# A hybrid SSD and attention encoder layer on one core: token statistics, V, dt and K at the start of the kernel

## The chip, the cores and the metric

The kernel runs on one core of one Trainium2 chip. Five engines work side by side and are tied together by semaphores: TensorE (PE in the profile, its weight loads PEld), VectorE (DVE), ScalarE (ACT), GpSimd (POOL) and SyncE (SP), which here only issues DMAs. The metric is the time of one execution on the device, in microseconds (us); lower is better. The time of a kernel is the median over its runs.

## The reference

One layer over 512 tokens of width 1024, in float32. Only its beginning matters here:

```python
h = rmsnorm(x, pre_mix_norm[l])          # x * rsqrt(mean(x*x) + EPS) * g
proj = h @ w_in[l]
z, xbc, dt_raw, q, k, v, gates = split_cols(proj, IN_SPLITS)
...
dt = jax.nn.softplus(dt_raw + dt_bias)   # 512 tokens x 64 (2 directions x 32 heads)
...
mixed = (g_ssd * y_ssd + g_attn * y_attn) @ w_o[l]
x = x + rmsnorm(mixed, post_mix_norm[l])
f = jnp.square(jax.nn.relu(rmsnorm(x, pre_mlp_norm[l]) @ w_mlp_in[l])) @ w_mlp_out[l]
x = x + rmsnorm(f, post_mlp_norm[l])
```

`rmsnorm` multiplies a token by one number of its own, r = rsqrt(mean(x*x) + EPS), and a channel by its gain g. Since r belongs to the token, (x * g * r) @ w equals ((x * g) @ w) * r: the factor can be put on before the product or after it. V has 256 columns, dt 64, K 256, Q 1024. The state-space scan and the windowed attention, two projections, a merge, an output projection and the MLP follow; they are most of the work, and nothing in them is changed.

## The kernel before

Every large product is one of float32 matrices in three passes: an operand is split into a high part `hi` (rounded to the format that TensorE multiplies in one pass, fp32r in the profile) and a low part `lo = x - hi`, and the helper `mm3` issues hi·hi, hi·lo and lo·hi into one PSUM bank. A plain float32 product (`mm` on unsplit operands) is also possible; TensorE makes it in several passes and it leaves two records in the trace for one instruction. Weights come by DMA into three buffers `wr` of 128x1024, ScalarE rounds them into `wh`, and GpSimd (for the first weights, DVE and GpSimd) subtracts to give `wl`; `wh` and `wl` have three buffers each too. Token tiles are 128x512, channels on the partitions: `h` holds, for each of the eight blocks k of 128 channels, the high and the low part of the normalised tokens. PSUM has eight banks, three with the tag `pp` and five with the tag `ps`.

The program is a list of quanta, each a product with the weight chunks it needs, and `at` hangs other work on a place in that list. When all is recorded, `Planner` sets the order of every engine's instructions: it simulates the program with a cost for each kind of instruction, takes TensorE's work in the order of the quanta (except that it may pick another ready product), and the others' by their due times; `chain` then ties the instructions of each engine together in that order. The order does not change at run time. SP may have eight DMAs under way; a further one waits for the landing of the one eight places earlier.

The start, around which the change lies:

- Eight products of ones keep TensorE busy while the first loads arrive.
- Tokens 0 to 255 come transposed from the host (`in_xt`, channels first, in five loads), and are multiplied by the gains into `xg` (L697 on ScalarE, L699 on DVE). The first quantum (`plain`) multiplies them, unsplit, with the raw V and dt weights `wr`: 16 plain float32 products of 320 columns, eight for each block of 128 tokens. Their result is multiplied by r at its eviction (L629, L630).
- All 512 tokens come once more as rows (`in_x`, eight loads of 128x512), because r needs the sum over a token's row: ScalarE and DVE sum the squares (L723, L724), GpSimd takes the power (L726, L727). Tokens 256 to 511 are scaled as rows and transposed on TensorE (16 products, L454) in `start_tokens`, then split with the gain into `h` (L475, L476). Their V and dt come from `rest`: 48 split products of 320 columns.
- Tokens 0 to 255 get their r in `scale_tokens`: GpSimd writes a diagonal matrix `dg` of r (L737), TensorE multiplies ones with it so that r stands in every partition of a bank (`rb`), DVE multiplies (L743), ScalarE rounds (L745) and GpSimd subtracts (L746) into `h`.
- Two K products follow (24 split products of 512 columns each, from `h`), then Q products of the same size, then the scores of the first head, which need K (`KH`, `KL`) and Q. K is split from its bank by `k_done`: L886 and L888 on ScalarE, L887 on DVE.
- `dt_math` makes the softplus of dt as |v|, exp, a reciprocal (L826), a product with it (L827) and a polynomial (L831 to L834), all in SBUF tiles of 128x256 called `dtw`.

Of the kernel before, what the change touches and what calls it, by code (L numbers as in the profile page):

```python
# [49 lines left out]
X_CHUNKS = ((0, 1), (1, 3), (3, 5), (5, 7), (7, 8))  # L50
COLD = 7000.0
RATE, EARLY, LAND = 260, 350, 2500
# [26 lines left out]
def packed(given):  # L79

    rows = lambda n: given[n].reshape(-1, 128)
    xt, wv = given["x"][0, :256].T.reshape(8, 128, 256), np.concatenate(
        [given["w_in"][0][:, c:c + n].reshape(8, 128, n) for c, n in ((C_V, 256), (C_DT, 64))], axis=2)
    pieces = lambda a, cuts: np.concatenate([a[k0:k1].transpose(1, 0, 2).reshape(-1) for k0, k1 in cuts])
# [9 lines left out]
    first = np.concatenate([rows("pre_mix_norm").T, xt[0]], axis=1)  # L94
    return {**{n + "_b": blocks(a) for n, a in mats.items()}, "cv": np.ascontiguousarray(cv), "row": row, "bias": bias,
            "xt": np.concatenate([first.reshape(-1), pieces(xt, X_CHUNKS[1:])]), "wv": pieces(wv, V_CHUNKS)}
# [21 lines left out]
class Planner:  # L118
# [191 lines left out]
    def plan(self, wait=0.3):  # L310
# [13 lines left out]
        for _ in self.ins:  # L324
# [22 lines left out]
            if e == "SP" or "DMA" in type(self.ins[n]).__name__:  # L347
                aps = self.operands(self.ins[n].outs)
                size = 4 * math.prod(d[1] for d in aps[0].ap)
                queue = max(queue, t + 900) + size / (EARLY if t < 12000 else RATE)  # L350
# [38 lines left out]
class Trunk:  # L389
# [206 lines left out]
    def v_quanta(self):  # L596
# [5 lines left out]
        self.dtv = get("dtw", (128, 4, 64))  # L602

        def chunk(k0, k1):
            kk = k1 - k0
            raw = []

            def loads():
                r = self.wp.tile([128, 1024], F32, tag="wr", name=self.name("wr"), bufs=RAW)
                self.tags[r.tensor.name] = "wr", RAW  # L610
                raw.append(r[:, :kk * 320].rearrange("p (k n) -> p k n", k=kk))
                (nc.sync if k0 else nc.scalar).dma_start(
                    r[:, :kk * 320], self.d_wv[k0 * 320 * 128:k1 * 320 * 128].rearrange("(p n) -> p n", p=128))

            def make():
                hi, lo = (t[:, :kk * 320].rearrange("p (k n) -> p k n", k=kk) for t in self.weight_parts())
                nc.scalar.copy(hi, raw[0])
                for k in range(kk):
                    e = nc.vector if k % 2 == 0 else nc.gpsimd
                    e.tensor_tensor(lo[:, k], raw[0][:, k], hi[:, k].bitcast(F32), op=ALU.subtract)  # L620
# [4 lines left out]
        def done(t, ps):  # L625
            bias = self.row[:, :64]
            if t < 2:
                r = self.rst0[:, t:t + 1]
                nc.scalar.activation(self.V[0][:, t], ps[:, :256], AF.Copy, scale=r)  # L629
                nc.vector.scalar_tensor_tensor(self.dtv[:, t], ps[:, 256:320], r, bias, op0=ALU.mult, op1=ALU.add)  # L630
            else:
                nc.scalar.copy(self.V[1][:, t - 2], ps[:, :256])
                nc.vector.tensor_tensor(self.dtv[:, t], ps[:, 256:320], bias, op=ALU.add)

        held, late = [], []

        def plain(parts):
            held.extend(parts)
            ps = [self.bank("ps") for _ in range(2)]
            for (k0, k1), (raw, _, _) in zip(V_CHUNKS, parts):  # L640
                for t in range(2):
                    for k in range(k0, k1):
                        self.mm(ps[t][:, :320], self.xg[k][:, tok(t)], raw[:, k - k0], k == 0, k == 7)
            for t in range(2):
                done(t, ps[t])

        def rest(c):
            def run(_):
                if c == 0:
                    late.extend(self.bank("ps") for _ in range(2))  # L650
                (k0, k1), (_, wh, wl) = V_CHUNKS[c], held[c]
                for t in (2, 3):
                    for k in range(k0, k1):
                        hi, lo = self.h[k]
                        self.mm3(late[t - 2][:, :320], (hi[:, tok(t)], lo[:, tok(t)]), (wh[:, k - k0], wl[:, k - k0]),
                                 k == 0, k == 7)
                if c == 2:
# [8 lines left out]
    def start(self):  # L666
# [21 lines left out]
        for x, (k0, k1) in zip(xt, X_CHUNKS):  # L688
# [3 lines left out]
            if k0 == 0:  # L692
                nc.vector.tensor_copy(self.gT, x[:, :8])
# [1091 lines left out]
```

## Time and profile before

| what | us |
|---|---|
| three runs | 1074.57, 1074.58, 1075.67 |
| median | 1074.58 |
| the profiled execution, whole | 1077.91 |
| its span, from the first to the last instruction of the program | 1076.1 |
| TensorE busy in that span | 1064.1 |

TensorE is busy for 99% of the span, at a granted clock of 0.998 of full speed. Its share of busy time says little of the others: DVE is at 71%, ScalarE at 61%, GpSimd at 74%. The 1.8 us between the span and the whole profiled execution lie around the program. The profiled execution is 3.3 us longer than the median of the runs; a difference worked out in its trace is taken over to the runs as it is.

How to read the rows that follow: a row of the timeline has the start and the duration in us, the engine, the line, the operation, what it writes and reads, the shape, how many instructions are merged in the row, and in brackets the idle time of that engine before it and what ended it. A row of the groups has, behind the bar, the busy time in us and the mean duration of one in ns, and then idle time. A row of the waits of TensorE has who waited for whom, the total in us, how often, and the longest. A row of the windows has the stretch, its length, and for each engine the busy time and the number of instructions.

### The profile page before, as it was taken

The page shows a single profiled execution, that of the slowest core. Times are in us where ns is not written, and L with a number is a line of the kernel's source. Part 1 is how long each engine was busy: PE and PEld are TensorE (multiplying, and loading weights), DVE is VectorE, ACT ScalarE, POOL GpSimd, SP SyncE. Part 2 cuts the span into 40 slices and gives each one's busy share as a digit, 9 for nine tenths or more (in the row PEclk, how much of TensorE's full clock was granted, in tenths as well). Part 3 has the DMA queues.
Part 4 walks back from the last instruction along what each step waited for, and adds up shares of the span by engine and source line. Part 5 has one row for each costly group of instructions (what it writes and reads, how often), then busy time and mean ns, then how long its engine had stood idle before and what let it go on. Part 6 is the DMA issues. An engine that isn't in the chain of part 4 may idle for free.

```text
span 1076.1 us, 16654 instructions
## 1 busy us (share of the span) xinstructions
PE 1064.1 (99%) x5542; PEld 895.0 (83%) x5542; DVE 769.1 (71%) x1363; ACT 657.7 (61%) x1409; POOL 797.6 (74%) x993
## 2 busy tenths in 40 slices
PE   9999999999999999999999999999999999999997
PEld 7788888888888888888888888889888888888885
DVE  5877778797786878788876626698663574574688
ACT  7676786786676767676777524466555444444552
POOL 5755548566677789899979976215587898898995
PEclk9999999999999999999999999999999999999999
DMA  8243324434434425254545544317221431424222
GB/s 290 90 140 92 119 91 116 131 98 110 124 123 122 152 89 186 84 142 143 147 128 153 161 154 155 108 53 271 89 69 60 156 97 61 157 90 151 73 98 78
DMA packets 61509, 133.20 MB, mean 124 GB/s; under 512 B 9064, under 2 KB 18920, under 8 KB 61424
## 3 DMA queue, kind: packets, MB, share of 16 engines
q1 hardware_dynamic: 61136, 131.76, 39.4%
q8 instruction: 43, 0.70, 0.3%
q14 instruction: 42, 0.34, 0.1%
q10 hardware_dynamic: 288, 0.39, 0.1%
HBM read 127.63 MB, written 4.49 MB: 123 GB/s over the span
## 4 chain that ended last, share of the span: by engine, by line
PE 91%; DVE 4%; ACT 2%; issue 1%; DMA 1%; POOL 0%; SPq 0%; DVEq 0%; POOLq 0%; ACTq 0%
PE pp L450 57%; PE ps L450 31%; PE ps L454 3%; DVE dtw L827 1%; DMA wr<-in_wv 1%; DVE u L1015 0%; ACT P L947 0%; DVE P L938 0%; DVE dtw L831 0%; PE pp L454 0%; DVE KL L887 0%; DVE P L953 0%; ACT h L745 0%; DVE x L1417 0%; DVE Q L914 0%
## 5 line engine op out<-in xcount | busy, mean ns | idle before, releaser
L529 POOL TENSOR_TENSOR wl<-wr,wh 128x256 fp32r<-128x256 f32 (+1 forms) x519 | 417.0, 835 | 168.7 <-ACT wh L525 166.0
L450 PE MATMUL pp<-h,wh 128*128 128x512 f32 (+1 forms) x1728 | 524.7, 385 | 1.2 <-ACT KH L888 1.2
L450 PEld LDWEIGHTS pp<-h,wh 128*128 128x128 f32 x1728 | 318.5, 188 | 63.2 <-ACT KH L888 1.6
L450 PE MATMUL pp<-h,wl 128*128 128x512 f32 (+1 forms) x864 | 333.9, 386 | 0.0
L525 ACT CAST wh<-wr 128x1024 fp32r<-128x1024 f32 (+1 forms) x130 | 135.4, 1041 | 126.5 <-PE pp L450 98.1
L450 PEld LDWEIGHTS pp<-h,wl 128*128 128x128 f32 x864 | 162.4, 188 | 31.9 <-issue 0.3
L1622 POOL TENSOR_TENSOR wl<-wd,wh 128x256 fp32r<-128x256 f32 x158 | 131.6, 870 | 11.9 <-ACT wh L1619 11.8
L1619 ACT CAST wh<-wd 128x512 fp32r<-128x512 f32 x92 | 53.2, 618 | 38.3 <-PE ps L450 22.1
L450 PE MATMUL ps<-wl,fh 128*128 128x512 f32 x184 | 71.7, 390 | 0.0
L450 PE MATMUL ps<-wh,fl 128*128 128x512 f32 x184 | 71.6, 389 | 0.0
L450 PE MATMUL ps<-wh,fh 128*128 128x512 f32 x184 | 71.6, 389 | 0.0
L1457 DVE SCALAR_TENSOR_TENSOR pp<-pp,r 128x256 f32<-128x256 f32 (+1 forms) x31 | 17.3, 559 | 65.5 <-ACT r L1454 65.4
L1181 ACT ACTIVATE n<-cb,tables 128x128 f32<-128x128 f32 x128 | 47.6, 391 | 16.4 <-DVE cb L1172 12.6
L1015 DVE SCALAR_TENSOR_TENSOR u<-pp,cv,u 128x510 f32<-128x510 f32 (+1 forms) x64 | 47.8, 746 | 9.7 <-ACT u L1011 8.4
L1220 POOL TENSOR_TENSOR w<-w,E 128x256 f32<-128x256 f32 x48 | 40.5, 859 | 16.3 <-DVE w L1216 15.3
L1182 ACT ACTIVATE m<-cb,tables 128x128 f32<-128x128 f32 x128 | 47.5, 389 | 7.2 <-DVE cb L1172 6.4
L1113 POOL TENSOR_TENSOR xd<-x,tables 128x256 f32<-128x256 f32 x48 | 32.5, 696 | 17.0 <-ACT x L1038 15.4
L1177 ACT ACTIVATE rf<-rf,tables 128x128 f32<-128x128 f32 x128 | 42.3, 392 | 3.3 <-DMA rf<-csT 3.2
L1175 POOL TENSOR_TENSOR rb<-rb,tables 128x512 f32<-128x512 f32 x32 | 36.5, 1142 | 10.0 <-DVE al L468 5.9
L947 ACT ACTIVATE P<-P,mx 128x384 f32<-128x384 f32 (+1 forms) x64 | 35.2, 552 | 14.0 <-DVE mx L944 14.0
L1674 DVE TENSOR_TENSOR acc<-acc,ps 128x512 f32<-128x512 f32 x46 | 31.3, 681 | 15.7 <-PE ps L450 15.5
L1183 DVE TENSOR_TENSOR m<-m,n 128x512 f32<-128x512 f32 x32 | 29.6, 925 | 16.0 <-ACT m L1182 15.5
(291 smaller groups left out, 2215.0 us busy)
## 6 DMA issues: line engine op xcount, KB each, us to landing
wr<-in_w_in_b SPq DMA_DIRECT2D x74, 512.0 KB, 3.9
wr<-in_w_mlp_in_b SPq DMA_DIRECT2D x32, 512.0 KB, 3.4
wd<-in_w_mlp_out SPq DMA_DIRECT2D x64, 256.0 KB, 4.5
rb<-csT SPq DMA_DIRECT2D x32, 256.0 KB, 3.8
rf<-csT SPq DMA_DIRECT2D x32, 256.0 KB, 3.8
wr<-in_w_ssd_out_b SPq DMA_DIRECT2D x13, 512.0 KB, 3.6
x<-in_x SPq DMA_DIRECT2D x16, 256.0 KB, 5.2
E<-csE SPq DMA_DIRECT2D x32, 128.0 KB, 4.5
```

Source lines behind the costliest of these rows:

```text
L450: self.nc.tensor.matmul(out, lhsT, rhs, start=start, stop=stop, skip_group_check=more)
L525: self.nc.scalar.copy(hi[:, :m], raw)
L529: engines[e].tensor_tensor(lo[:, c], raw[:, c], hi[:, c].bitcast(F32), op=ALU.subtract)
L947: nc.scalar.activation(p[:, :w], p[:, :w], AF.Exp, bias=mx[:, n:n + 1], accum_out=sm[:, n:n + 1])
L1015: nc.vector.scalar_tensor_tensor(u[:, a:e], ps[:, a + d:e + d], self.wtap(t, b), u[:, a:e], op0=ALU.mult, op1=ALU.add)
L1175: nc.gpsimd.tensor_tensor(v4(rb), v4(rb), cs[:, 1].unsqueeze(2).to_broadcast([128, 4, 128]), op=ALU.subtract)
L1177: nc.scalar.activation(v4(rf)[:, h], v4(rf)[:, h], AF.Identity, bias=ncs[:, 0, h:h + 1])
L1181: nc.scalar.activation(v4(n)[:, h], cb[:, 0], AF.Copy, scale=dt[:, 0, h:h + 1])
L1182: nc.scalar.activation(v4(m)[:, h], cb[:, 1], AF.Copy, scale=dt[:, 1, h:h + 1])
L1220: nc.gpsimd.tensor_tensor(wc, wc, E[:, d], op=ALU.add)
L1619: nc.scalar.copy(hi, src)
L1622: (nc.vector if q == 512 else nc.gpsimd).tensor_tensor(lo[:, c], src[:, c], hi[:, c].bitcast(F32), op=ALU.subtract)
```

## The change

Seven edits, all within the start:

1. All 512 tokens come transposed from the host: eight loads of 128x512 (`xt`), one for each block of 128 channels. The gains travel with the first V and dt weights, which come in four loads instead of three (`W_CHUNKS`).
2. ScalarE and DVE split each transposed block, multiplied by the gain but not by r, into a second set of operands `hr` (hi and lo, all 512 tokens; `raw_tokens`). The transposes on TensorE and `start_tokens` are gone.
3. V and dt of all four token blocks come from `hr`: for the first channel block by four plain products (`PLAIN = 1`), for the other seven by 84 split ones; all four banks are multiplied by r at their eviction. The V weights are rounded block by block.
4. The K products read `hr` too. `k_done` first multiplies the bank by r into a tile `kf` on DVE, and splits K from there.
5. `scale_tokens` now makes `h` for all 512 tokens: four `dg` on DVE instead of two on GpSimd; DVE multiplies each `xt` by its gain and the bank `rb` (128x512), ScalarE rounds, and GpSimd (even k, two halves) or DVE (odd k, whole) subtracts. It is placed after the V products, and `rb` is also copied to SBUF for K.
6. The identity, which `dg` needs, is now issued on SP after the first weights of K instead of on ScalarE at the beginning.
7. In `dt_math` the tiles `e` and `s2` lie in a PSUM bank, and one step writes to another tile than before; the computation is the same.

The planner's numbers for early DMAs change with it (350 to 370 bytes per ns, up to 20 us instead of 12 us).

```diff
-V_CHUNKS = ((0, 2), (2, 5), (5, 8))
-X_CHUNKS = ((0, 1), (1, 3), (3, 5), (5, 7), (7, 8))
+W_CHUNKS = ((0, 1), (1, 2), (2, 5), (5, 8))
+PLAIN, SCALE_AT = 1, 2.5
...
+        def product(k0, k1):
+            def run(parts):
+                if k0 == 0:
+                    banks.extend(self.bank("ps") for _ in range(4))
+                raw, wh, wl = parts[0]
+                for k in range(k0, k1):
+                    for t in range(4):
+                        ps = banks[t][:, :320]
+                        if k < PLAIN:
+                            self.mm(ps, self.xg[k][:, tok(t)], raw[:, k - k0], k == 0, k == 7)
+                        else:
+                            hi, lo = self.hr[k]
+                            self.mm3(ps, (hi[:, tok(t)], lo[:, tok(t)]), (wh[:, k - k0], wl[:, k - k0]), k == 0, k == 7)
+                if k1 == 8:
+                    for t in range(4):
+                        done(t, banks[t])
                     self.dt_math()
...
-        self.at(0, lambda: nc.scalar.dma_start(self.ident, self.d_cst[:, :128]))
+        self.at(0, lambda: nc.sync.dma_start(self.ident, self.d_cst[:, :128]))
...
+    def raw_tokens(self):
+        nc = self.nc
+        for k, x in enumerate(self.xt):
+            g = self.gT[:, k:k + 1]
+            if k < PLAIN:
+                for c in (slice(0, 256), slice(256, 512)):
+                    nc.vector.tensor_scalar(self.xg[k][:, c], x[:, c], self.g0 if k == 0 else g, None, op0=ALU.mult)
+            hi, lo = self.hr[k]
+            self.split_by(hi, lo, x, g)
+        for t in range(4):
+            xt = self.load_tokens(t)
+            self.token_scale(t, xt)
...
-        for t in range(2):
+        for t in range(4):
             dg = get("dg", (128, 128))
-            nc.gpsimd.tensor_scalar(dg, self.ident, self.rst0[:, t:t + 1], None, op0=ALU.mult)
+            nc.vector.tensor_scalar(dg, self.ident, self.rst0[:, t:t + 1], None, op0=ALU.mult)
             self.mm(rb[:, t * 128:(t + 1) * 128], ones, dg, True, True)
...
+        self.rb = get("rb")
+        nc.scalar.copy(self.rb, rb)
         for k in range(8):
...
+            x = self.xt[k]
+            hi, lo = self.h[k]
+            nc.vector.scalar_tensor_tensor(x, x, self.gT[:, k:k + 1], rb, op0=ALU.mult, op1=ALU.mult)
             nc.scalar.copy(hi, x)
...
+            for e, c in ((nc.vector, slice(0, 512)),) if k % 2 else ((nc.gpsimd, slice(0, 256)), (nc.gpsimd, slice(256, 512))):
+                e.tensor_tensor(lo[:, c], x[:, c], hi[:, c].bitcast(F32), op=ALU.subtract)
...
-        w = [self.dtv] + [get("dtw", (128, 4, 64)) for _ in range(5)]
-        v, e, r, s2, p, al = w
+        w = [self.dtv] + [get("dtw", (128, 4, 64)) for _ in range(3)]
+        v, r, p, al = w
+        bank = self.bank("ps")
+        e, s2 = (bank[:, a:a + 256].rearrange("p (c h) -> p c h", c=4) for a in (0, 256))
...
         def k_done(ps):
+            x = get("kf")
+            nc.vector.tensor_tensor(x, ps, self.rb, op=ALU.mult)
             for j in range(2):
...
-                nc.scalar.copy(KH[a], ps[a])
-                nc.vector.tensor_tensor(KL[a], ps[a], KH[a].bitcast(F32), op=ALU.subtract)
+                nc.scalar.copy(KH[a], x[a])
+                nc.vector.tensor_tensor(KL[a], x[a], KH[a].bitcast(F32), op=ALU.subtract)
...
-        hh = lambda: self.h
+        hh = lambda: self.hr
```

Where the order moves. First place, the beginning of the program on TensorE: the products behind the ones, before (`ps` banks of tokens 0 to 127 and 128 to 255, raw weights `wr`):

```order
L450 MATMUL pp_82<-ones_80 128x128 x8
L450 MATMUL ps_177<-wr_153,xg_113 128x320
L450 MATMUL ps_178<-wr_153,xg_113 128x320
L450 MATMUL ps_177<-wr_153,xg_113 128x320
L450 MATMUL ps_178<-wr_153,xg_113 128x320
L450 MATMUL ps_177<-wr_155,xg_114 128x320 x2
```

and after (four banks, one for each 128 tokens; `hr_109` and `hr_110` are the high and low part of the second channel block):

```order
L452 MATMUL pp_82<-ones_80 128x128 x8
L452 MATMUL ps_229<-wr_142,xg_132 128x320
L452 MATMUL ps_230<-wr_142,xg_132 128x320
L452 MATMUL ps_231<-wr_142,xg_132 128x320
L452 MATMUL ps_232<-wr_142,xg_132 128x320
L452 MATMUL ps_229<-wh_150,hr_109 128x320
L452 MATMUL ps_229<-wl_151,hr_109 128x320
L452 MATMUL ps_229<-wh_150,hr_110 128x320
```

Split products now stand where plain ones stood, from the fifth product on, and need ScalarE's and DVE's parts there.

On SP the loads between the tokens' rows and the constants, before (`row` is dt's bias and other small vectors, broadcast; `wr` the weights of K and Q):

```order
L715 DMA x_142<-in_x 128x512
L435 DMA row<-in_row 128x176
L505 DMA wr_199<-in_w_in_b 128x1024
L505 DMA wr_312<-in_w_in_b 128x1024
L921 DMA bt_501<-in_bias 128x384
```

and after:

```order
L709 DMA x_220<-in_x 128x512
L507 DMA wr_249<-in_w_in_b 128x1024
L667 DMA ident<-in_cst 128x128
L507 DMA wr_251<-in_w_in_b 128x1024
L507 DMA wr_299<-in_w_in_b 128x1024
L437 DMA row<-in_row 128x176
```

The identity stands behind the first weights of K, and `row` behind those of K and of the first Q product.

Second place, the softplus and K on DVE. Before (`dtw_376` is e, `dtw_377` the reciprocal, `pp_409` the first K bank, `dtw_71` dt before the softplus):

```order
L743 TENSOR_TENSOR hf_271<-pp_261,xg_116 128x256 x2
L633 TENSOR_TENSOR dtw_71<-ps_299,row 128x64
L826 RECIPROCAL dtw_377<-dtw_377 128x256
L827 TENSOR_TENSOR dtw_376<-dtw_376,dtw_377 128x256
L887 TENSOR_TENSOR KL_435<-pp_409,KH_434 64x512
L887 TENSOR_TENSOR KL_441<-pp_409,KH_440 64x512
L831 SCALAR_TENSOR_TENSOR dtw_379<-dtw_379,dtw_378 128x256 x5
```

After (`ps_358` is the bank of e and s2; `pp_378` the bank `rb`; `h_94`, `h_98`, `h_102`, `h_106` the low parts of odd channel blocks):

```order
L739 SCALAR_TENSOR_TENSOR xt_131<-xt_131,gT,pp_378 128x512
L742 TENSOR_TENSOR h_94<-xt_125,h_93 128x512
L742 TENSOR_TENSOR h_98<-xt_127,h_97 128x512
L742 TENSOR_TENSOR h_102<-xt_129,h_101 128x512
L639 SCALAR_TENSOR_TENSOR dtw_71<-ps_232,rst_79,row 128x64
L742 TENSOR_TENSOR h_106<-xt_131,h_105 128x512
L860 TENSOR_TENSOR kf_458<-pp_433,rb_391 128x512
L803 RECIPROCAL dtw_355<-dtw_355 128x256
L804 TENSOR_TENSOR ps_358<-ps_358,dtw_355 128x256
L866 TENSOR_TENSOR KL_461<-kf_458,KH_460 64x512
L809 SCALAR_TENSOR_TENSOR dtw_356<-dtw_356,ps_358 128x256 x6
```

Four subtractions of 128x512 with both operands in SBUF stand ahead of K and the softplus; the subtraction for `KL` reads SBUF instead of a bank.

On GpSimd at the same place, before:

```order
L737 TENSOR_SCALAR dg_265<-ident,rst_79 128x128
L529 TENSOR_TENSOR wl_315<-wr_199,wh_314 128x256 x4
L746 TENSOR_TENSOR h_92<-hf_268,h_91 128x256
L746 TENSOR_TENSOR h_94<-hf_268,h_93 128x256
L746 TENSOR_TENSOR h_96<-hf_269,h_95 128x256
```

and after (`wl_254` and `wl_302` are K's, `wl_424` and `wl_475` those of the first two Q products):

```order
L531 TENSOR_TENSOR wl_254<-wr_249,wh_253 128x256 x4
L531 TENSOR_TENSOR wl_302<-wr_251,wh_301 128x256 x4
L742 TENSOR_TENSOR h_92<-xt_124,h_91 128x256 x2
L531 TENSOR_TENSOR wl_424<-wr_299,wh_423 128x256
L742 TENSOR_TENSOR h_96<-xt_126,h_95 128x256 x2
L531 TENSOR_TENSOR wl_424<-wr_299,wh_423 128x256
L742 TENSOR_TENSOR h_100<-xt_128,h_99 128x256 x2
L531 TENSOR_TENSOR wl_424<-wr_299,wh_423 128x256
```

K's low parts come first now, and `h` is made between the weights of the first Q product. Behind the scores of the first head, TensorE's products stand in the same order in both programs to the end.

154 lines of the change are left out of this document (51 added, 103 removed).

## The prediction

> **What bounds the kernel now.** I read the page first, then TensorE's waits, then its windows, then the timeline of the first 50 us.
>
> ```profile
> span 1076.1 us, 16654 instructions
> ...
> PE 1064.1 (99%) x5542; PEld 895.0 (83%) x5542; DVE 769.1 (71%) x1363; ACT 657.7 (61%) x1409; POOL 797.6 (74%) x993
> ```
>
> ```profile
> PE pp L450 <- ACT KH L888: 1.2, 1, 1.2
> PE ps L450 <- DVE pT L964: 1.1, 1, 1.1
> ...
> PE ps L450 <- DVE Q L914: 0.3, 1, 0.3
> ```
>
> ```profile
> 4.62:25.27 20.65, 20.08 (x102) 15.79 (x102) 14.18 (x36) 15.41 (x36) 12.22 (x19) 1.00 0.85 313
> 25.27:49.00 23.73, 22.24 (x98) 17.75 (x96) 18.29 (x22) 15.04 (x28) 17.51 (x25) 1.00 0.26 88
> 49.00:1076.10 1027.10, 1018.24 (x5330) 857.84 (x5330) 736.03 (x1302) 625.12 (x1345) 767.68 (x947) 1.00 0.39 121
> ```
>
> Behind each stretch stand its length and TensorE's busy time. TensorE bounds the kernel from 5 us to the end. From the first head's scores (49.00) on its order is the same in both programs, so the change is worth what it moves that moment; the 1027.1 us behind it are taken over unchanged. Two stretches lie ahead: to the first K product (25.27), and two K and two Q products to the scores.
>
> ```profile
> 1.04 3.79 PE L450 MATMUL pp<-ones 128*128 128x128 f32 x16 [1.04 <-DVE two L675]
> 4.62 10.33 PE L450 MATMUL ps<-wr,xg 128*128 128x320 f32 x32
> 15.14 0.44 PE L454 MATMUL pp<-ident,x 128*128 128x128 f32 x2 [0.20 <-ACT x L760]
> ...
> 16.78 0.38 PE L454 MATMUL ps<-ident,x 128*128 128x128 f32 x2
> ...
> 20.28 0.46 PE L450 MATMUL ps<-wh,h 128*128 128x320 f32 x2
> ...
> 22.04 0.46 PE L450 MATMUL ps<-wh,h 128*128 128x320 f32 x2
> ...
> 22.77 0.61 PE L450 MATMUL pp<-dg,ones 128*128 128x128 f32 x4
> ...
> 25.27 0.62 PE L450 MATMUL pp<-h,wh 128*128 128x512 f32 x2
> ...
> 49.00 0.39 PE L450 MATMUL ps<-KH,Q 128*128 128x256 f32 x1 [0.30 <-DVE Q L914]
> ```
>
> ```profile
> 5.15 0.34 PEld L450 LDWEIGHTS ps<-wr,xg 128*128 128x128 f32 x1 [0.20 <-issue]
> 5.68 0.34 PEld L450 LDWEIGHTS ps<-wr,xg 128*128 128x128 f32 x1 [0.20 <-issue]
> ```
>
> A plain product of 320 columns takes 0.53 us (5.15 to 5.68), a split one 0.147 (twelve between 20.28 and 22.04). The first stretch holds 16 x 0.53 = 8.5, the transposes (15.14 to 17.1) 2.0, 48 x 0.147 = 7.1 and two `dg` products, at most 0.6: 18.2 us of work in 20.65; the other 2.4 are waits for loads and for r. In the second stretch 1.5 us are waits (1.2 and 0.3). Their cause:
>
> ```profile
> 29.93 8.42 POOL L529 TENSOR_TENSOR wl<-wr,wh 128x256 fp32r<-128x256 f32 x12
> 30.02 1.75 DVE L826 RECIPROCAL dtw<-dtw 128x256 f32<-128x256 f32 x1 [1.64 <-ACT dtw L825]
> ...
> 31.81 7.17 DVE L827 TENSOR_TENSOR dtw<-dtw,dtw 128x256 f32<-128x256 f32 x1
> ...
> 38.90 0.67 DVE L887 TENSOR_TENSOR KL<-pp,KH 64x512 fp32r<-64x512 f32 x1
> 39.61 0.58 ACT L888 CAST KH<-pp 64x512 fp32r<-64x512 f32 x1 [7.14 <-DVE KL L887]
> ```
>
> L827 takes 7.17 us and ends when GpSimd's unbroken run of twelve subtractions (0.70 each) is over. K's low part stands behind it on DVE, ScalarE behind that, and TensorE lacks the next rounded weights.
>
> **The change: TensorE's own work.** Twelve plain products go (6.4 us), 36 split ones come (5.3); the transposes go (2.0), two `dg` products come (at most 0.6). 15.7 against 18.2: 2.5 us less, certain as far as TensorE stays the bound.
>
> **Loads.** The rows of the windows give what the DMAs moved.
>
> ```profile
> 0.00:5.00 5.00, 3.96 (x17) 3.92 (x18) 0.87 (x6) 2.20 (x3) 0.41 (x5) 1.00 0.64 197
> 5.00:10.00 5.00, 4.86 (x15) 2.97 (x14) 3.13 (x6) 2.46 (x5) 2.12 (x2) 1.00 1.01 373
> 10.00:15.00 5.00, 4.94 (x19) 3.17 (x17) 3.51 (x9) 3.95 (x9) 2.82 (x5) 1.00 1.05 386
> 15.00:20.00 5.00, 4.62 (x32) 4.04 (x33) 4.31 (x14) 4.70 (x14) 3.33 (x7) 1.00 1.03 397
> ```
>
> ```profile
> 13.58 0.63 ACT L723 ACTIVATE junk<-x 128x512 f32<-128x512 f32 x1 [0.63 <-DMA x<-in_x]
> 14.12 0.18 ACT L723 ACTIVATION_READ_ACCUMULATOR junk<-x 128x1 f32 x1
> 14.36 0.72 ACT L760 ACTIVATE x<-x,rst 128x512 f32<-128x512 f32 x1
> ```
>
> 0.98 MB are moved by 5 us, 2.85 by 10, 4.78 by 15, 6.77 by 20. ScalarE waits until 13.57 for the fifth load of rows; by the queue's order 3.74 MB stand up to its end, but 4.23 had been moved, so a load lands when 0.49 MB more than its place in the queue have gone. After: the transposed tokens are 2.10 MB, the V weights 1.31, the rows 2.10, K's first weights 0.52, the identity 0.07. SP's limit of eight holds each load until the one eight places ahead has landed, which keeps some 2 MB under way, as before. The last rows land at 5.51 + 0.49 MB: 18.1 us; K's weights at 19.4; the identity, now behind them, at 19.6; `row`, behind two more weights, at 22.6. The eight blocks land early enough: block k+1 and its weights need about 0.43 MB, 1.1 us, and TensorE takes 12 x 0.147 = 1.76 us for a block.
>
> **The parts for V.** A block costs ScalarE 0.72 (L760, 512 columns times a column) and a third of a rounding of 960 columns, DVE a multiply-and-subtract of 128x512 and mostly one subtraction for the weights, GpSimd the others.
>
> ```profile
> 9.86 0.99 ACT L617 CAST wh<-wr 128x960 fp32r<-128x960 f32 x1 [0.74 <-DMA wr<-in_wv]
> ```
>
> ```profile
> 4.79 1.17 POOL L620 TENSOR_TENSOR wl<-wr,wh 128x320 fp32r<-128x320 f32 x1 [4.36 <-ACT wh L617]
> ```
>
> ```profile
> L1183 DVE TENSOR_TENSOR m<-m,n 128x512 f32<-128x512 f32 x32 | 29.6, 925 | 16.0 <-ACT m L1182 15.5 <-ACT n L1181 0.4
> ...
> L1022 DVE SCALAR_TENSOR_TENSOR u<-th,u 128x512 f32<-128x512 f32 x16 | 15.2, 949 | 2.1 <-ACT th L1021 2.1
> ...
> L1457 DVE SCALAR_TENSOR_TENSOR pp<-pp,r 128x512 f32<-128x512 f32 x15 | 10.5, 697 | 43.6 <-ACT r L1454 43.6
> ```
>
> ScalarE: about 1.1 us a block; DVE: 0.95 (L1022, both operands in SBUF) and some 0.5: 1.45; both under TensorE's 1.76, so only the first blocks can wait. TensorE begins at 4.6 as before, since the ones end there, finishes four plain products at 6.75, and the second block's low part on DVE comes at about 7.3, the third's weights at about 9.3. I take 0.9 us of waits (0.2 if all parts are early; 3.5 if each of seven blocks waits 0.5): V ends at 6.75 + 12.35 + 0.9 = 20.0.
>
> **r, `dg`, the start of K.** The last rows land at 18.1.
>
> ```profile
> 12.37 0.68 DVE L724 CUSTOM_DVE_ANT_0 junk<-x 128x512 f32<-128x512 f32 x1
> ...
> 13.20 0.51 POOL L726 TENSOR_TENSOR rst<-ssq 128x1 f32<-128x1 f32 x1 [1.10 <-DVE ssq L724]
> 13.79 0.54 POOL L727 TENSOR_TENSOR rst<-rst,mhalf 128x1 f32<-128x1 f32 x1
> 14.37 0.48 DVE L761 TENSOR_SCALAR x<-x,rst 128x512 f32<-128x512 f32 x1 [0.70 <-POOL rst L727]
> ```
>
> DVE's sum takes 0.7, GpSimd 0.5 and 0.54: the last r stands at 19.8, 0.2 behind the identity. Four `dg` on DVE take less than L761's 0.48 for 512 columns; at 0.3 each, begun at 19.6, they end at 20.8 (between 20.4 and 21.5), the last product at 21.1. The sum waits here, not in V: **K begins at 21.1 instead of 25.27**, 4.2 us earlier. Its weights (19.4, and a rounding of about 1.05) are there at 20.5, GpSimd's first quarter of low parts at 21.2, when TensorE's third product needs it.
>
> **K, `h` and Q.** The stretch to the scores keeps its 22.24 us of products; L827's 1.5 us go, if its successor with an operand in a bank does not wait for GpSimd: it reads a bank as L1457 does (0.70 for 512 columns, so 0.4 here). What is late next is `h` for the first Q product, at 21.1 + 11.0 = 32.1. DVE makes eight products from the bank (0.70) from 21.1 on, held once by `row` until 22.6: done at 28.5; four subtractions at 0.93 (L1183): 32.2, needed at 32.8, 34.2, 35.5 and 36.9. GpSimd has 24 subtractions ahead of the second Q product, 24 x 0.70 = 16.8 from 20.5 on, plus up to four times 0.93 when DVE's take turns with them: 37.3 to 41.0. The last quarter of the first Q product's weights comes 2.8 earlier, at 34.5 to 38.2, and is needed at 36.7. I take 0.3 us of waits (0 to 1.5). From 32.2 DVE has K's new multiply (0.70), the reciprocal (1.75), the product with it (0.4), a subtraction for K now from SBUF (up to 0.93), six polynomial steps (0.4, at most 0.7), the second multiply and the first Q's eviction (0.70 each): 39.8 to 41.6, some 2 us ahead of the scores. That slack hides the edits to K; without it each multiply costs its 0.70. ScalarE's copy of `rb` (about 0.7) and its five more roundings lie beside eleven us of K products and beside V, and delay nothing that TensorE waits for within 1 us. Scores: 21.1 + 22.24 + 0.3 = 43.6, against 49.0: **5.4 us** earlier.
>
> **The sum** is against the profiled execution, 1077.91 us with a span of 1076.1; the median of the runs is 1074.58. 1074.58 - 5.4 = **1069.2 us** (the profiled one: 1072.5). Its own range takes the bounds above: `dg` at its best (K at 20.7), no waits, and the 1.1 us before the values (L964) gone too give 7.2 us, 1067.4; V waiting 3.5, with four `dg` products behind it, starts K at 23.8, and with 1.5 in Q 1.5 us are left, 1073.1.
>
> **Rivals.**
>
> *The load sets the start.* With 1.0 MB more ahead of r (4.53 to 5.51), the rows land 2.5 us later. Were the rate behind 5 us 330 bytes per ns instead of 385, the identity would land at 22.0 and K begin at 23.5: 3.0 us gained, 1071.6. For: the DMA share is 1.0 throughout, and SP holds only eight loads under way. Against: the 373 to 397 hold for 15 us with the same sizes of load.
>
> *The softplus still waits.* Its reciprocal still lies in SBUF. If the product after it waits for GpSimd's run to end (39.3), the first Q is evicted about 1 us after the scores could start: 4.3 us gained, 1070.3. Against: L1457, with a bank operand, averages 0.697 over 15.
>
> *DVE starves at `h`.* The four subtractions read two SBUF tiles, like L827, and GpSimd runs unbroken from 20.5 to 37.3. If DVE only comes in when that run ends, the second block's low part is there at 38.1 instead of 29.4, TensorE idles 5.3 us, and K and the softplus, all behind it, let the scores start at 48.7: 0.3 us gained, 1074.3. [...] The 32 of L1183 average 0.93 beside GpSimd's work, so I hold to the sum.
>
> *The same stall, and TensorE cools.* This one ends slower. The ones at the beginning took 3.79 us for eight products, 0.47 each, where `dg` took at most 0.3: TensorE starts slow. If 5.3 us of idleness bring that back, the first Q product goes on at half rate for 3.8 us up to its whole rest of 4.6 us of work, which loses 1.9 to 4.6 us: 1076.2 to 1078.9, middle 1077.5. It decides, against 1074.58, from 0.3 us lost on top of the stall. [...]
>
> **Chances.** Forecast 0.64; load 0.13; softplus 0.09; starved 0.07; starved and cool 0.07. A measurement tells 0.2% (2.15 us) from no change: 1072.4 to 1076.7. The first three lie below that but for 0.02 of the load: faster 0.84, same 0.09, slower 0.07. From 1066.8 to 1073.5, which adds to the forecast's own range 0.6 us for loads that run ahead of these windows and 0.4 above, about 0.05 is left out below and 0.14 above.
>
> **What would show it.** Right: K's first product near 21, no DVE row of several us by the softplus, scores near 43.6, about 1027 us behind them. Wrong: the four subtractions for `h` with rows over 2 us; TensorE waiting for `hr` in V over 2 us together; a wait for `dg` past 22; a granted clock under 1.0 before 50 us; or a stretch behind the scores longer than 1027.1.

## The result

The changed kernel took 1079.83 us, the median of 22 runs, against 1074.59 for 22 runs of the kernel before beside them: the ratio is 1.0031, with a 95% interval of 1.0016 to 1.0046. It is slower by 0.3%; 1069.2 was forecast, and the upper end of the range was 1073.5.

The median hides two kinds of execution, and without that the rest can't be understood: of the 34 executions of the changed kernel (22 here, and ten and two single ones below), 11 lie from 1072.1 to 1075.4, three from 1076.3 to 1077.2, and 20 from 1079.4 to 1087.0. The eleven have a median of 1073.38. The profiled one took 1073.35 and is of the first kind. TensorE's waits in it, the windows from the first V product to the end, some of VectorE's timeline, and the first products of K and of the scores:

```profile
span 1071.5 us, 16667 instructions
```

```profile
PE ps L452 <- DVE pT L946: 1.3, 1, 1.3
PE pp L452 <- DVE dg L731: 1.1, 3, 0.8
```

```profile
4.62:22.20 17.58, 16.48 (x99) 14.82 (x98) 12.87 (x25) 13.04 (x27) 8.15 (x14) 1.00 1.04 389
22.20:44.49 22.29, 22.28 (x100) 18.51 (x101) 20.39 (x34) 18.50 (x35) 21.00 (x27) 1.00 0.48 146
44.49:1071.50 1027.01, 1017.94 (x5331) 857.59 (x5329) 738.39 (x1305) 626.74 (x1346) 767.27 (x947) 1.00 0.38 120
```

```profile
20.32 1.84 DVE L731 TENSOR_SCALAR dg<-ident,rst 128x128 f32<-128x128 f32 x4 [1.44 <-DMA ident<-in_cst]
...
29.20 3.38 DVE L742 TENSOR_TENSOR h<-xt,h 128x512 fp32r<-128x512 f32 x3
...
36.17 0.43 DVE L804 TENSOR_TENSOR ps<-ps,dtw 128x256 f32<-128x256 f32 x1
```

```profile
22.45 0.71 PE L452 MATMUL pp<-hr,wh 128*128 128x512 f32 x2
...
44.33 0.28 PE L452 MATMUL ps<-KH,Q 128*128 128x256 f32 x1
```

Here the change does what it says: softplus's product takes 0.43 us where it took 7.17, h's first three subtractions 3.38 together, K's first product starts at 22.45 and the scores stand at 44.3, 4.7 us ahead of the profile of before (the windows are cut at the last of rb's products and in the first of the scores'). Two things are wrong with taking that for the gain. This execution isn't the usual one, and, as a later experiment shows, neither was the profiled one of before.

The first scores product and the time from it to the end (rest) measure all traces alike (us):

| trace | first K product | first scores product | rest | span |
|---|---|---|---|---|
| before, profiled | 25.27 | 49.00 | 1027.1 | 1076.1 |
| before, a second execution | 25.10 | 46.88 | 1025.5 | 1072.4 |
| changed, profiled | 22.45 | 44.33 | 1027.1 | 1071.5 |
| changed, again_a | 22.46 | 44.35 | 1030.9 | 1075.3 |
| changed, again_b | 22.43 | 44.33 | 1029.9 | 1074.3 |
| changed, of ten more | 22.21 | 51.10 | 1028.6 | 1079.7 |

### The profile page after: what moved, and what is told of

It is laid out like the page before. It is cut to its first block, busy times and chain, and to the rows that moved or that the text cites. A ratio compares the mean times of both kernels' runs of the same rounds, so it can differ in the third digit from the quotient of the medians.

```text
span 1071.5 us, 16667 instructions
## 1 busy us (share of the span) xinstructions
PE 1060.3 (99%) x5542; PEld 894.5 (83%) x5542; DVE 772.4 (72%) x1368; ACT 660.1 (62%) x1408; POOL 796.6 (74%) x991
## 4 chain that ended last, share of the span: by engine, by line
PE 95%; DMA 2%; DVE 1%; ACT 1%; issue 0%; SPq 0%; POOL 0%; DVEq 0%; POOLq 0%; ACTq 0%
PE pp L452 61%; PE ps L452 31%; PE ps L456 3%; DMA ident<-in_cst 1%; DMA x<-in_x 1%; DMA wr<-in_wv 1%; DVE x L1399 0%; ACT wh L527 0%; ACT P L929 0%; DVE P L920 0%; DVE acc L1378 0%; DVE dg L731 0%; PE pp L456 0%; DVEq L1763 0%; DVE ag L1678 0%
## 5 line engine op out<-in xcount | busy, mean ns | idle before, releaser
L452 PE MATMUL pp<-h,wh 128*128 128x512 f32 (+1 forms) x1696 | 514.6, 385 | 0.0
L452 PEld LDWEIGHTS pp<-h,wh 128*128 128x128 f32 x1696 | 312.6, 188 | 60.5 <-issue 0.5
L452 PE MATMUL pp<-h,wl 128*128 128x512 f32 (+1 forms) x848 | 327.6, 386 | 0.0
L452 PEld LDWEIGHTS pp<-h,wl 128*128 128x128 f32 x848 | 159.4, 188 | 31.2 <-POOL wl L531 0.2
```

The lines of the kernel that those rows point to most:

```text
L452: self.nc.tensor.matmul(out, lhsT, rhs, start=start, stop=stop, skip_group_check=more)
```

## The experiments

**Two more executions of the changed kernel** (again_a and again_b). No edit.

> The changed kernel once more, unaltered, to look into another of its executions: of its timed runs about eight in 22 lie at 1072.1 to 1073.7 us and twelve at 1079.4 to 1085.1. Theory 1, TensorE's clock: in an execution of the second kind the granted clock is under 1.0 for some us ahead of 60 us, and the stretch from 4.6 us to the first head's scores, 39.9 us in the one already seen, is longer by 6 to 12 us, with the 1027.0 us behind it unchanged. Theory 2, VectorE starves: one subtraction of the start that is 0.85 us long takes over 4 us, as that one of 7.17 us did before, TensorE has a wait for VectorE of 3 us or more there, and the time is 1076 to 1080. Theory 3, the loads: the transfers of the first 20 us land later by 2 us or more and V is that much longer. If the extra time lies behind 60 us, all three fall.

> A second look of the same kind, with the same three readings: under the clock theory the stretch from 4.6 us to the scores is 39.9 us or 46 to 52; under the starving theory one row of VectorE of over 4 us stands in it; under the loads theory the first landings are late by 2 us or more.

1077.23 and 1076.34 us. In both the scores start at 44.3, as in the profiled execution; the extra time lies behind them, so all three theories fall as they were put. In the first, 612 us into the program, VectorE's subtraction for the MLP's input meets an unbroken run of GpSimd's:

```profile
611.90 6.64 DVE L1301 TENSOR_TENSOR yl<-yT,yh 128x512 fp32r<-128x512 f32 x1 [6.02 <-ACT yh L1300]
```

```profile
611.74 0.73 POOL L1210 TENSOR_TENSOR ssq<-sq 128x256 f32<-128x256 f32 x1
612.44 5.56 POOL L531 TENSOR_TENSOR wl<-wr,wh 128x192 fp32r<-128x192 f32 x9
```

The same instruction form took 0.67 us at its fastest in this trace. It ends at 618.54, half a microsecond behind GpSimd's ninth subtraction, and TensorE waits 2.6 us for it. So the hold that the prediction knew from L827 is not tied to the start. In the second most of the extra time is the clock's, told at the end.

**The softplus part alone** (softplus_only), in the kernel before.

```diff
-        w = [self.dtv] + [get("dtw", (128, 4, 64)) for _ in range(5)]
-        v, e, r, s2, p, al = w
+        w = [self.dtv] + [get("dtw", (128, 4, 64)) for _ in range(3)]
+        v, r, p, al = w
+        bank = self.bank("ps")
+        e, s2 = (bank[:, a:a + 256].rearrange("p (c h) -> p c h", c=4) for a in (0, 256))
...
```

> The kernel before with the first part of the change alone: e and s2 of softplus in a PSUM bank. My forecast's term for it: the 7.17 us product goes, TensorE's 1.50 us of wait with it, and the time falls by 1.0 to 2.0 us, to about 1073. The rival that TensorE's wait has another end close behind gives no change (under 0.3 us). A rival for the spread: if the PSUM product is what varies from run to run, these runs spread over 6 us or more as the changed kernel's do; by the clock theory they spread over under 1.5 us, as the kernel before does.

1075.11 us (10 runs) against 1075.58 (13): 0.9992, interval 0.9977 to 1.0008. The interval, from 2.5 us lower to 0.9 higher, doesn't rule out the expected 1.0 to 2.0. But the runs under 1077 are alike (eight of each, medians 1074.97 and 1074.84): in an ordinary execution there is nothing to gain, and one traced has its first scores product at 46.96. Five of the 13 runs of the kernel before lay above 1077 here and two of these ten, too few to tell a difference of shares. Those two have no trace; in the one traced the product, now with an operand in a bank, takes 0.43 us.

**The changed kernel in ten more executions** (after_many). No edit.

> The changed kernel unaltered, in more executions and beside variants on the same chip. By what the two looks showed (a subtraction of the start of the MLP, 1.05 us long, took 6.64 us behind nine GpSimd instructions, and V to K 0.5 us more), the extra time is one-sided and drawn anew in each execution: a lowest time within 1 us of 1072.1, and other executions 2 to 8 us above it. If it is the start of the kernel that starves (theory 2a), the executions above 1076 have a row of over 3 us at the four subtractions of h or the four of KL; if any VectorE subtraction of two SBUF operands beside GpSimd is exposed (theory 2b), the long row is elsewhere. Clock theory: no such row, and the granted clock under 1.0 behind the pause before K.

1072.79 to 1087.04, median 1080.38; seven of ten at 1080.0 or above. Its trace is of the one that took 1081.66 us, and shows where most of the loss is. TensorE's waits, L742's instructions on VectorE (their number, then the shortest, the median and the longest in ns), the timelines of GpSimd and TensorE, and the windows around the pause (the third number from the end is the granted clock):

```profile
PE pp L452 <- DVE h L742: 4.9, 1, 4.9
PE ps L452 <- DVE pT L946: 2.0, 1, 2.0
```

```profile
L742 DVE TENSOR_TENSOR h<-xt,h x4: 676/680/9484, 29.6 to 40.4; 128x512 fp32r<-128x512 f32 x4
```

```profile
29.54 1.46 POOL L742 TENSOR_TENSOR h<-xt,h 128x256 fp32r<-128x256 f32 x2
30.93 0.77 POOL L531 TENSOR_TENSOR wl<-wr,wh 128x256 fp32r<-128x256 f32 x1
31.63 1.46 POOL L742 TENSOR_TENSOR h<-xt,h 128x256 fp32r<-128x256 f32 x2
33.02 0.77 POOL L531 TENSOR_TENSOR wl<-wr,wh 128x256 fp32r<-128x256 f32 x1
33.71 1.45 POOL L742 TENSOR_TENSOR h<-xt,h 128x256 fp32r<-128x256 f32 x2
35.08 3.48 POOL L531 TENSOR_TENSOR wl<-wr,wh 128x256 fp32r<-128x256 f32 x5
```

```profile
39.16 0.79 PE L452 MATMUL pp<-h,wh 128*128 128x512 f32 x1 [4.87 <-DVE h L742]
```

```profile
35.00:36.00 1.00, 0.00 (x0) 0.00 (x0) 1.00 (x1) 0.00 (x0) 1.00 (x3) 1.00 0.41 109
36.00:37.00 1.00, 0.00 (x0) 0.00 (x0) 1.00 (x1) 0.00 (x0) 1.00 (x2) 0.63 0.37 33
37.00:43.00 6.00, 3.84 (x9) 3.06 (x10) 5.60 (x7) 2.40 (x6) 1.56 (x3) 0.50 0.52 169
43.00:44.00 1.00, 1.00 (x5) 0.80 (x5) 0.97 (x2) 0.23 (x1) 0.00 (x0) 0.96 0.00 0
```

The first of the four subtractions, begun at 29.6, lasts 9.48 us: twelve whole GpSimd instructions pass it, and it is through half a microsecond after the last of them (38.56). TensorE stands still for 4.87, the granted clock falls to 0.50 meanwhile, and the products go on at half speed from 39.16 until about 43.1, which costs half of 3.9 us. 4.87 + 1.95 account for the 6.8 us by which the scores are late (51.10 against 44.33); the other 1.4 us lie behind them, 0.7 in the wait for pT.

Hold and clock are the prediction's last rival, "the same stall, and TensorE cools", in its place, with 4.9 us of idleness for the 5.3 it gave and 1.95 for its lower bound of 1.9.

**h's subtractions with an operand in PSUM** (h_psum).

```diff
-            nc.vector.scalar_tensor_tensor(x, x, self.gT[:, k:k + 1], rb, op0=ALU.mult, op1=ALU.mult)
+            y = self.bank("ps") if k % 2 else x
+            nc.vector.scalar_tensor_tensor(y, x, self.gT[:, k:k + 1], rb, op0=ALU.mult, op1=ALU.mult)
+            x = y
```

> The changed kernel, with x g rstd of the odd k written to a PSUM bank by VectorE, and h's two parts made from there, so that the four whole-width subtractions of h read one PSUM operand; the rest of the program stands as it did but for a few places near them. Theory 2a (h starves at the start): the group of 1079 to 1085 is gone, all executions lie within 2 us of 1072 but for those that KL holds. Theory 2b (exposed anywhere): the spread stays as in the unaltered kernel of the same call, within what ten executions tell. Clock theory: no change of the spread. In each the lowest time stays within 1 us of 1072.1.

1079.08 to 1080.70 in all four runs. The expectation of a return to 1072 fails, by its own exception: the hold moved on to the next VectorE instruction with two SBUF operands, KL.

```profile
34.37 6.53 DVE L868 TENSOR_TENSOR KL<-kf,KH 64x512 fp32r<-64x512 f32 x1
```

```profile
33.98 6.30 POOL L531 TENSOR_TENSOR wl<-wr,wh 128x256 fp32r<-128x256 f32 x9
```

It too is through 0.6 us after GpSimd's nine subtractions (40.28). The four subtractions of h, a little earlier beside the same engine's work, are not held:

```profile
29.26 2.48 DVE L744 TENSOR_TENSOR h<-ps,h 128x512 fp32r<-128x512 f32 x4
```

The span of this execution is 8.3 us longer than that of hk_psum below, where nothing is held, but the scores are only 1.6 later (45.80 against 44.23). The other 6.8 lie behind them: VectorE takes the first scores from their bank 5.7 us later (50.41 against 44.66), TensorE then waits 3.1 us for pT, which it doesn't in hk_psum, and its clock is halved for 3.4. That this is the hold of KL carried on by VectorE is read from these times, not tested apart.

**More products of ones ahead of V** (warm24), against a clock that falls.

```diff
-WARM = 8
+WARM = 24
```

> The changed kernel with 24 products of ones ahead of V in place of 8, so that TensorE is busy for 3 to 4 us more before it could pause. Clock theory (the gate falls in the start because the products that keep it up are few): the executions above 1076 become rare, and the lowest time rises by the 2 to 4 us by which V begins later. Theories 2a and 2b: the spread stays and all times rise by 2 to 4 us.

1078.42 to 1087.49, median 1086.85; V begins 3.9 us later, K 1.4. The spread doesn't go, so a clock that falls for want of products at the start isn't the cause. The trace has h held for 10.95 us, past 15 GpSimd instructions, and TensorE waiting 7.6.

**h and KL both from PSUM** (hk_psum): the edit of h_psum, and

```diff
-            x = get("kf")
+            x = self.bank("ps")
             nc.vector.tensor_tensor(x, ps, self.rb, op=ALU.mult)
...
```

> The changed kernel with both exposed kinds of subtraction fed from a PSUM bank: h of the odd k as in h_psum, and K times rb written to a bank too, so that KL reads PSUM. Theory (VectorE's subtractions of two SBUF operands are held until GpSimd's unbroken run ends, whichever comes first in it): with none left ahead of the first head's scores, TensorE has no wait of over 2.5 us and no granted clock under 1.0 there, the group of 1079 and above is gone, and the time is 1071 to 1075, up to 3 us of it from the planner's other order around softplus. Rival (a hold moves on to whatever VectorE does next, as it moved from h to KL in h_psum, or the loss was the later order): the times stay at 1079 to 1081.

1072.27 us (12 runs, 1071.68 to 1075.30) against 1074.75 of the kernel before (23 runs): 0.9970, interval 0.9956 to 0.9983. No run lies in the upper group. TensorE's waits and the stretch to the scores in its profile:

```profile
PE pp L452 <- DVE dg L731: 1.1, 3, 0.7
PE pp L452 <- DVE two L671: 1.0, 1, 1.0
```

```profile
22.34:44.23 21.89, 21.89 (x99) 18.11 (x98) 19.93 (x36) 16.98 (x34) 18.59 (x27) 1.00 0.54 165
44.23:1069.98 1025.75, 1017.96 (x5331) 857.72 (x5329) 733.77 (x1301) 626.26 (x1347) 768.03 (x947) 1.00 0.38 120
```

Only `dg` and the start (`two`) are waited for. This version beats both kernels. The 23 runs of the kernel before include eight above 1077; against the median of the other 15, 1074.17, the ratio is 0.9982. The order of VectorE moved with the edit, though: the reciprocal of the softplus, at 34.38 behind h's subtractions in the changed kernel, stands ahead of them at 28.41. So the time by itself doesn't part operands from order; for the operands speak the traces, in which no instruction fed from a bank is held. A second execution of it, unaltered in spite of its name (hk_early_ident):

> The kernel of hk_psum unaltered, for a second look at an execution of it beside the next one: one time within 1071.6 to 1075.3.

1073.72 us. Some 360 us behind the scores a VectorE product (L1166, 0.68 us at its shortest) is held for 4.08: the places behind the scores are as exposed as ever.

**rb's products amid K's first block** (hk_late_rb), on hk_psum.

```diff
-PLAIN, SCALE_AT = 1, 2.5
+PLAIN, SCALE_AT = 1, 3.5
```

> hk_psum with the products of rb placed amid K's first block instead of ahead of it, so that K need not wait for dg: K's products wait for nothing but their own weights. If the pause ahead of K (1.1 us for dg in the changed kernel's profile, and the 0.7 us of rb's products as they stand in it) is on the path, the time falls by 0.5 to 2 us against hk_psum. If h is late for Q instead (its chain starts with rb, and in this order softplus stands ahead of it on VectorE), TensorE waits for h by 1 to 4 us and the time is not lower, or higher by as much.

1080.28 us (12 runs, 1078.98 to 1084.03). K does begin 1.8 us earlier than in hk_psum (20.53 against 22.34), and all is lost again, more than expected: h is late.

```profile
PE pp L452 <- DVE ps L740: 7.2, 1, 7.2
```

```profile
37.00:44.00 7.00, 3.64 (x9) 2.90 (x10) 6.94 (x12) 4.32 (x9) 5.89 (x9) 0.53 0.15 61
```

Nothing is held here; VectorE works through softplus before most of h, and from 27.4 us on it is never idle for more than 0.2 us before h is done. The pause alone, without any hold, brought the half clock here (0.53 over this window): the two causes are told apart.

**The identity early** (hk_ident), on hk_psum.

```diff
-        self.at(0, lambda: nc.sync.dma_start(self.ident, self.d_cst[:, :128]))
+        self.at(0, lambda: nc.scalar.dma_start(self.ident, self.d_cst[:, :128]))
```

> hk_psum with the identity loaded on ScalarE's queue at the beginning, as the kernel before has it, in place of behind the rows and K's first weights: by the changed kernel's profile dg began 20.32, released by that load (landed 20.22), with the last r at 20.04. If the load is what K waits for, three dg stand before the last r, K begins 0.8 to 1.5 us earlier and the time falls by as much, to about 1071. If r alone sets it, or the 64 KB ahead push the rows back by as much, the change is under 0.4 us.

1072.51 us (12 runs) against hk_psum's 1072.27 on another chip: no gain, as the second reading had it. Three `dg` do stand earlier, but the last ends no sooner:

```profile
18.18 0.29 DVE L731 TENSOR_SCALAR dg<-ident,rst 128x128 f32<-128x128 f32 x1 [0.70 <-POOL rst L721]
18.39 0.68 DVE L718 CUSTOM_DVE_ANT_0 junk<-x 128x512 f32<-128x512 f32 x1
...
21.61 0.74 DVE L731 TENSOR_SCALAR dg<-ident,rst 128x128 f32<-128x128 f32 x1 [0.49 <-POOL rst L721]
```

Now r is late. VectorE's `dg` stand between its sums of squares, the rows land about 1.1 us later (ScalarE's last square, which its row releases, starts at 18.41, in hk_psum at 17.34), and r's power on GpSimd takes 1.08 beside those sums where it took 0.55 alone.

**A second execution of the kernel before** (before_look). No edit.

> The kernel before, unaltered, to look into one of its ordinary executions: the profiled one took 1077.91 us, the median of its runs 1074.58, and my sum took L827's wait of 1.5 us off the median. If the held product of softplus (7.17 us) is in every execution, this one has it too at about 1074.5, and the 3.3 us between profile and median lie elsewhere. If the hold is drawn anew each time, as it is in the changed kernel, an execution at 1074.5 has no row of over 2 us there, TensorE's waits of the second stretch are under 0.6 us, and the gain that was forecast is too large by 1.5 us or more already at its base.

1074.25 us, an ordinary execution. The window from K to the scores, and the timelines of VectorE and GpSimd:

```profile
25.10:46.88 21.78, 21.78 (x98) 18.03 (x97) 16.08 (x23) 16.40 (x30) 21.33 (x28) 1.00 0.36 120
```

```profile
29.85 1.75 DVE L826 RECIPROCAL dtw<-dtw 128x256 f32<-128x256 f32 x1 [1.64 <-ACT dtw L825]
31.64 0.56 DVE L827 TENSOR_TENSOR dtw<-dtw,dtw 128x256 f32<-128x256 f32 x1
```

```profile
29.77 9.35 POOL L529 TENSOR_TENSOR wl<-wr,wh 128x256 fp32r<-128x256 f32 x12
```

The same product, behind the same reciprocal and beside the same twelve GpSimd subtractions, takes 0.56 instead of 7.17. TensorE waits for nothing in K and Q, and the scores start at 46.88. The hold is drawn anew in each execution. Times above 1077 us, as the profiled one of before, come in a share that differs between the series: 0 of 22 runs of the kernel before, 5 of 13, 0 of 15, 8 of 23, 9 of 17 and 1 of 11; the 15 and the 23 ran on the same chip. That all of them have the softplus held isn't shown.

**The softplus part undone** (hk_sbuf_softplus), on hk_psum: e and s2 in SBUF again, so that this part alone is exposed.

```diff
-        bank = self.bank("ps")
-        e, s2 = (bank[:, a:a + 256].rearrange("p (c h) -> p c h", c=4) for a in (0, 256))
+        w = [self.dtv] + [get("dtw", (128, 4, 64)) for _ in range(5)]
+        v, e, r, s2, p, al = w
...
```

> hk_psum with softplus's e and s2 back in SBUF as in the kernel before: the first part of the change undone where nothing else is exposed. Theory (any VectorE operation on two SBUF operands can be held to the end of GpSimd's run): its product and ten multiply-and-adds are exposed again, beside GpSimd's subtractions; a part of the executions has a row of 3 us or more among them and lies 2 to 8 us above the others, which stay at 1071.7 to 1073. Rival (the softplus has slack enough, or its hold in the kernel before came from the reciprocal's place alone): all executions within 1071.7 to 1075.3, as those of hk_psum.

1077.80 to 1081.13 in all six runs, 1.0039 of the kernel before (interval 1.0025 to 1.0053).

```profile
34.91 6.68 DVE L804 TENSOR_TENSOR dtw<-dtw,dtw 128x256 f32<-128x256 f32 x1
```

```profile
34.99 6.32 POOL L531 TENSOR_TENSOR wl<-wr,wh 128x256 fp32r<-128x256 f32 x9
```

The hold is back at the softplus's first product. The scores are 2.4 us later than in hk_psum (46.66 against 44.23), behind a wait of 2.5 for Q; the other 4.3 us lie behind them, with waits for pT (1.5) and KH (0.8) and 3.4 us at half clock. In the traces with a hold ahead of the scores, it is the first of the exposed places left, h, KL or the softplus, that has it.

## Why the prediction was wrong

**TensorE bounds the kernel; the order behind the scores is the same: right.** 1027.1 us stood behind the scores, as taken over. But that is no constant: 1025.5 to 1025.9 in traces without disturbance, up to 1032.5 with it. That the two profiled executions agree is luck: each holds a wait for pT, of 1.1 and 1.3 us.

**The base of the sum: wrong.** The prediction took 5.4 us, found in an execution of 1077.91 us, off a median of 1074.58. It named the 3.3 us between them and didn't ask where they lay. In the ordinary execution of before_look, 3.7 us shorter, L827 isn't held and the scores start at 46.88 and not at 49.00. So 2.1 us lay in the very term that the prediction then removed, and had never been in the median; the other 1.5 lie behind the scores, 1.1 of them in the wait for pT.

**V, r and `dg`: right in kind, 1.35 us too early.** V ended at 19.9 (20.0), the last r stood at 20.04 (19.8). The identity landed at 20.22 (19.6) and the four `dg` took 1.84 us (1.2): the first two 0.29 and 0.28, the last two, beside GpSimd's first subtractions for K, 0.76 and 0.77. K's first product came at 22.45 instead of 21.1. The load did not set the start, as one rival had it (389 bytes per ns in the window to 22.2, for its 330); the identity was late for `dg` by 0.2 us.

**The price of a plain product: right by luck.** The two rows that give 0.53 us are 0.53 apart, but they belong to two successive records, and a product leaves two: at the slow start, up to 6.75 us, it takes 1.07. From 7.1 us on the records are 0.27 apart, which makes 0.54 a product. So of the 2.4 us put down as waits, 1.1 are the slow start; TensorE's records leave only 0.6 us of that stretch idle (20.08 busy of 20.65).

**K to the scores: right, where nothing was held.** 21.9 us against 22.54.

Together: 46.88 - 44.33 = 2.55 us gained where no instruction is held, instead of 5.4. From 1074.59 that gives 1072.0, where the changed kernel's fastest executions (1072.1) and hk_psum's median (1072.27) lie. The profiled execution lost 1.6 of it again behind the scores.

**The four subtractions for h: the step that failed.** The prediction took them at 0.93 from the average of L1183, and gave the hold 0.14 in two rivals. The average was the wrong row: in each of the 14 traces some 260 VectorE instructions with two SBUF operands begin inside one of GpSimd's, and all but one at most are through within 1.6 us; seven traces have one that is passed by all that stand back to back. What counts is whether that one falls where TensorE needs it. 20 of 34 executions lost 7 us or more; the one of them traced has a subtraction of 9.48 us there, for the 0.93 of the sum. The rival was priced from the right rows (4.9 of 5.3 us idle, 1.95 of 1.9 to 4.6 lost to the clock), but came out at 1077.5 in its middle; set on an undisturbed 1072, with 6.8 us to the scores and 1.4 behind, it is the 1080 of the median.

**The softplus's move to a bank: right, and worth nothing in the median.** The bank does keep it from being held (0.43 us in the profiled execution; undone, 6.68 in the one traced, and all six runs at 1077.8 or more). The change removed this exposure and put two new ones in its place: h's odd k, which GpSimd had made before, and KL, which had read PSUM.

**Left open:** what decides whether VectorE gets in. It isn't an even chance: of the seven holds five fall into the first 45 us, where only 1 to 11 of those 260 instructions stand. In again_b the subtraction of h began 0.09 us into a GpSimd instruction with 0.65 left and waited for that one; in the one of 1081.66 us it began 0.09 into the same instruction, 0.68 left, and was passed by twelve. Nor is it known why the share differs between the series, on one chip too. For the other 19 executions above 1079 the place of the hold is argued from their times and lower mean clock (0.992 to 0.997, against 0.997 to 0.999), not shown. To break GpSimd's run up instead of moving VectorE's operands wasn't tried.

## What to carry to other kernels

A single profile is one draw: before taking a term off the median, look whether the profiled execution is itself off the median, and whether the term is what sets it apart. Of the VectorE instructions on two SBUF operands that began inside one of GpSimd's, some 260 in each of the 14 traces, all but one at most were through within 1.6 us; seven in all waited for GpSimd's run and took 4.08 to 10.95 us. Where TensorE waits for such a one, give it an operand in PSUM (in hk_psum none of 12 runs took more than 1075.30 us), all such places of a stretch at once, since in h_psum the hold went to the next one, of 6.53 us. Removing one stall is worth what the undisturbed execution shows, and a new exposure has to be priced by its worst row, not its average.

## What the runs showed of the hardware

**A held VectorE instruction waited for the run, not for one instruction.** Seven holds past more than one GpSimd instruction are in the traces. Besides the one in progress when VectorE's began, these passed it whole: nine (L827 before), 12 and 15 (h), eight (KL), nine (L1301), nine (L804), four (L1166). Each is through within 0.7 us of the last instruction of GpSimd's run. The other instructions of that kind, some 260 in each trace, were through within 1.6 us.

**The half clock followed pauses of 1.82 us and more, and not all of them.** In again_b TensorE waited 1.82 us for pT, and the clock was down for 3.4 us behind that:

```profile
77.27 0.44 PE L452 MATMUL ps<-KH,Q 128*128 128x384 f32 x1 [1.82 <-DVE pT L946]
```

```profile
77.00:78.00 1.00, 0.73 (x4) 0.73 (x5) 0.94 (x4) 0.97 (x3) 0.18 (x1) 0.96 0.62 188
78.00:81.00 3.00, 3.00 (x10) 2.51 (x9) 2.43 (x8) 0.44 (x2) 1.04 (x1) 0.50 0.60 181
81.00:82.00 1.00, 1.00 (x5) 0.77 (x5) 0.00 (x0) 1.00 (x5) 0.00 (x0) 0.83 0.00 0
```

0.56 us more of pause than in the profiled execution, and half of 3.4 us of products, make 2.3 of its extra 2.8 us. Pauses of 1.26 us in the profiled execution and 1.47 in again_a at the same place left the clock alone, and so did one of 1.97 in the execution of 1081.66 us. One of 3.12 in h_psum brought it down for as long, and one of 3.19 us in warm24 did not:

```profile
84.08 0.45 PE L452 MATMUL ps<-KH,Q 128*128 128x384 f32 x1 [1.97 <-DVE pT L946]
```

```profile
88.97 0.44 PE L452 MATMUL ps<-KH,Q 128*128 128x384 f32 x1 [3.19 <-DVE pT L946]
```

```profile
90.00:94.00 4.00, 4.00 (x21) 3.27 (x20) 2.27 (x8) 1.63 (x6) 1.04 (x1) 1.00 0.32 122
```

Ahead of TensorE's last products six traces have a stretch at half clock (0.50), one each. It lasted 3.4 us in again_b (77.9 to 81.3), h_psum (81.7 to 85.1) and hk_sbuf_softplus (48.8 to 52.2), and 6.8 us, twice that, in the execution of 1081.66 us (36.3 to 43.1), warm24 (39.5 to 46.3) and hk_late_rb (37.4 to 44.2). The 6.8 us go with the longer waits, of 4.9, 7.6 and 7.2 us; the 3.4 us with 1.82, 3.12, and 2.5 followed by 0.75. But the length of a pause doesn't tell whether the clock falls: behind 1.82 us it was down, behind 1.97 and 3.19 not. What else decides it isn't shown.
